# New spacings in a kernel's own planner, and a list of dense items in another order

## The chip, the cores and the metric

One core of one Trainium2 chip runs the whole program. The time is device microseconds of one execution, as a median over several runs. A profile is one execution of its own; its views give times in us from the span's start. TensorE is also called PE, VectorE DVE, ScalarE ACT, GpSimd POOL, SyncE SP.

## The reference

Two layers of a transformer over 256 latent tokens and 256 context tokens of 1024 channels, in float32. Cut to what matters here:

```python
for l in range(DEPTH):                                   # DEPTH = 2
    m_lat, m_ctx = (cond @ w_mod[l] + b_mod[l] for cond in (silu(c), silu(c_ctx)))   # 6 x 1024 each
    h = modulate(rmsnorm(x or ctx, norm1_g[l]), shift1, scale1)
    p = h @ w_in[l]          # q, k, v of three mixers, and 3 x 1024 gates
    ya = attention(GQA, 8 heads of 64 on 2 key heads, rotary)
    yb = neighbourhood attention (8 heads, bias) ; context keys in the same softmax
    yc = attention(MLA, 8 heads, keys and values from a latent of 256)
    y = (g0 * (ya @ w_o_gqa) + g1 * (yb @ w_o_na) + g2 * (yc @ w_o_mla)) @ w_out[l]
    x = x + gate1 * y
    x = x + gate2 * (square(relu(modulate(rmsnorm(x, norm2_g[l]), shift2, scale2) @ w_mlp1[l])) @ w_mlp2[l])
    # the context tokens go the same way in layer 0 alone
return rmsnorm(x, final_norm_g)
```

Latent queries read latent and context keys, context queries read context keys alone. Layer 1 computes only the latent stream to its end.

## The kernel before

**Matmuls.** A float32 product is made of three matmuls of fp32r operands: each operand is split into a high part (a cast on ACT) and a low part (a subtraction on DVE), and `mm3` (L762 to L764) adds high·high, high·low and low·high in one PSUM bank. Activations are stored transposed, channels on partitions; a contraction over 1024 channels is eight chunks of three matmuls. In layer 0 most have 512 columns (latent and context tokens), in layer 1 256.

**Weights** lie in DRAM as tiles of 128 x 1024, in the order of their use. SP issues one DMA per tile into a raw buffer (three of their own, `raw`, and others lent from the arena of slots, `s`); ACT casts it into `wh` (L699), DVE makes `wl` (L700), and the raw buffer is free again. There are three pairs of `wh` and `wl` (wh_69 with wl_70, wh_71 with wl_72, wh_73 with wl_74); an item called "more" lends further pairs from the arena, "less" takes them back.

**Modulation.** The 16 half tiles of shift and scale of layer 0's first norm (items c0 to c7) are used by TensorE straight from the raw buffer (L835), with a selecting matmul behind each pair (L845); chunk c of the normalized input waits for item c. The other 80 tiles (items w) are reduced by DVE (L905).

**Attention.** A unit is a pair of heads: four of neighbourhood attention (NA), four of MLA, four of GQA per layer, in this order. For every half of 128 queries a job makes scores (L1524, L1525; for MLA L762 to L764 with 96 rows), a maximum (L1639 to L1651), an exponential on ACT (L1667), a scaling on DVE or ACT (L1678 or L1676, whichever the planner finds free first), four transposes (L1696), a cast and a subtraction (L808, L809), and then the group's weighted sum (L1730, L1731). MLA's heads are put together by DMAs on POOL's queue (L1405, L1407, L1409).

**What sets the order.** The program is built by a planner. `SEQ` names, for each layer, the dense items in the order in which they get their slots and weights: qN, kN, vN, aN, lN, ckv, rope are projections for NA, GQA and MLA, gXN and oXN gate and output tiles of a mixer, yX and sX its result buffers and their splitting, "attn" gives attention its buffers, "norm", W and M are the second norm, the output projection and the MLP. Every item and every attention job is a coroutine that asks for an engine with a cost in us. The planner keeps its own rough clock: when an engine is free in it, the waiting request with the best key is issued, and so stands next in that engine's queue. The chip's queues run in that order, each stopping at an instruction whose inputs are not there. A cost does nothing else than to move instructions. The costs and the hop between engines:

```python
    def post(self, th, cmd):
        ...
            key = (th.pri, th.order, self.seq) if e == "pe" else (self.now + slack, th.order, self.seq)
    def dispatch(self):
        ...
                cost = w[1] * (2 if e == "pe" and self.now < COLD else 1)
                self.busy[e] = self.now + cost
```

On TensorE attention's jobs come ahead of dense items (`pri` −1 against 1), and dense items fill what is left.

Of the kernel before, what the change touches and what calls it, by code (L numbers as in the profile page):

```python
# [30 lines left out]
GA, NA, ML = range(3)  # L31
# [34 lines left out]

BR = {"N": NA, "L": ML, "G": GA}
SEQ = (
# [7 lines left out]
)  # L76


# [314 lines left out]

class Planner:
    ENGINES = ("pe", "act", "dve", "pool", "hw", "dma")
    HOP = 0.15

    def __init__(self):
        self.now, self.seq = 0.0, 0
# [40 lines left out]
    def step(self, th, val=None):  # L440
        while True:
            try:
                cmd = th.gen.send(val)
            except StopIteration:
                self.live -= 1
                self.threads.remove(th)
                return
            val = None
            th.cmd = cmd
            k = cmd[0]  # L450
            if k in self.pend or k == "any":
                hop = self.HOP if th.eng != k else 0.0
                th.eng = k
                self.at(self.now + hop, lambda: self.post(th, cmd))
                return
            if k == "wait":
                if not cmd[1].on:
                    th.eng = None
                    cmd[1].waiters.append(th)
                    return  # L460
            elif k == "get":
                self.seq += 1
                cmd[1].waiters.append((th.pri, th.order, self.seq, th, cmd[2]))
                self.serve(cmd[1])
                return
            elif k == "sleep":
                th.eng = None
                self.at(self.now + cmd[1], lambda: self.step(th))
                return
            else:  # L470
                raise ValueError(k)
# [73 lines left out]
class Prog:  # L545
# [138 lines left out]
    def transfer(self, n):  # L684

        yield ("sleep", 0.65)
        yield ("dma", n * 1.422e-3, lambda: None)
        yield ("sleep", 1.2)

    def arrive(self, i, r, n):  # L690
# [75 lines left out]
    def acc(self, out, a, b):  # L766

        def get(o):
            if isinstance(o, Opnd):
                yield from o.wait()  # L770
                return o.hi, o.lo
            if callable(o):
                return (yield from o())
            return o

        n = 1
        for d in out.shape[1:]:
            n *= d
        for k in range(len(a)):
            x = yield from get(a[k])  # L780
            y = yield from get(b[k])
            yield ("pe", 3 * max(n, 256) / 2400.0 + (0.0128 if n <= 256 else 0.0093),
                   lambda: self.mm3(out, x, y, k == 0, k == len(a) - 1))

    @staticmethod
# [104 lines left out]
    def it_wm(self, l, part, fc, mem):  # L890
# [11 lines left out]
        for j in range(nj):  # L902
            for h in range(2):
                r = slice(h * 512, (h + 1) * 512)
                yield from self.dve(512, lambda: nc.vector.tensor_tensor_reduce(  # L905
                    self.junk, w[0][:, r], self.crow[j][:, r], 1.0, 0.0, ALU.mult, ALU.add,
                    accum_out=acc[1][:, fc, j, h:h + 1]), SL_M)
        self.give_raw(w)
# [710 lines left out]
    def job(self, l, g, qt, qleaf):  # L1619
# [7 lines left out]
        def score():  # L1627
            if lat:
                make(sc, slice(qt * P, qt * P + P), slice(0, T))
            else:  # L1630
                for a in range(2):
                    make(sc[:, a * 256:(a + 1) * 256], slice(NLAT + a * P, NLAT + a * P + P), slice(NLAT, T))
        yield ("pe", 0.645 if br == ML else 0.43, score)
        for f in qleaf:
            f.done()
        sm = self.pool_c.tile([P, 6], F32, tag="sm", bufs=8, name=self.nm("sm"))
# [4 lines left out]
        elif br == NA:  # L1641
# [4 lines left out]
            def mx():  # L1646
# [2 lines left out]
                nc.vector.tensor_scalar(pt[:, 256:512], sc[:, 256:512], 1.0, None, ALU.mult, ALU.max,  # L1649
                                        accum_out=sm[:, 5:6])  # L1650
                nc.vector.tensor_scalar(sm[:, 0:1], sm[:, 4:5], sm[:, 5:6], -1.0, ALU.max, ALU.mult)  # L1651
            yield ("dve", 0.9, mx)
            src = pt
            self.bias_n[h] = self.bias_n.get(h, 0) + 1
            if self.bias_n[h] == 2:
# [8 lines left out]
        def ex():  # L1664
            for a in range(m):
                r = slice(a * w, (a + 1) * w)
                nc.scalar.activation(pt[:, r], src[:, r], AF.Exp, bias=sm[:, a:a + 1], accum_out=sm[:, 2 + a:3 + a])  # L1667
        yield ("act", 0.62 + 0.15 * (m - 1), ex)
        if src is sc:
            self.unbank(bank)  # L1670

# [21 lines left out]
        def tr():  # L1693
# [3 lines left out]
            else:  # L1697
                for c in range(2):
                    for a in range(2):
                        nc.tensor.transpose(ps[:, c * 256 + a * P:c * 256 + (a + 1) * P],  # L1700
                                            pt[:, a * 256 + c * P:a * 256 + (c + 1) * P], self.ident)
        yield ("pe", 0.443, tr)
        self.pl.give(self.pbuf, pt)
        hi, lo = g["prob"]
        if lat:
# [11 lines left out]
    def pv(self, l, g):  # L1717
# [9 lines left out]
        for k0 in range(0, nk, 2):  # L1727
            def fn():
                for k in (k0, k0 + 1):
                    mm(ps, v[o + k], hi[:, k, :], start=k == 0, stop=False)  # L1730
                    mm(ps, v[o + k], lo[:, k, :], start=False, stop=k == nk - 1)  # L1731
            yield ("pe", 0.443, fn)
        self.pl.give(self.prob, g["prob"])
        for f in g["vleaf"]:
            f.done()
# [436 lines left out]
```

## Time and profile before

| | |
|---|---|
| median of 3 runs | 1458.03 us (1457.59 to 1458.78) |
| the profiled execution | 1459.33 us, span 1457.6, granted clock 0.991 |
| PE, DVE, ACT busy | 97%, 74%, 52% of the span |
| DMA | 210.91 MB, mean 145 GB/s |

A row of grouped instructions gives line, engine, operation, operands by the program's names, shape and count; a timeline's row start, length and, in brackets, the idle time before it with what ended it; a row of stretches each engine's busy time with its number of instructions. TensorE's work follows the list: the start to about 45 us, layer 0's projections and units to about 420, its output projection, norm and MLP to about 850, and the same for layer 1, whose units lie between 965 and 1190 and whose second norm is near 1257.

### The profile page before, as it was taken

Reading aid. Unit: us, or ns where it says so; the run is one execution under the profiler, and the core shown is the slowest. Engines: PE = TensorE matmul, PEld = TensorE weight load, DVE = VectorE, ACT = ScalarE, POOL = GpSimd, SP = SyncE. Lnnn points to the kernel's source line nnn. Section 1 sums busy time; section 2 is a strip of 40 time slices with the busy share of each in tenths; the row PEclk is TensorE's granted clock in tenths of the full one; section 3 lists DMA queues with packets and bytes.
Section 4 is the critical chain, followed back from the end, with each engine's and each line's share of the span. In section 5 each row is a group of like instructions: output and inputs, shape, how many; then the busy total and the mean of one; then the engine's idle time right before and its main releaser. Section 6 shows DMA issues by size and latency. Waiting matters only on the chain.

```text
span 1457.6 us, 23967 instructions
## 1 busy us (share of the span) xinstructions
PE 1419.6 (97%) x9294; PEld 1290.2 (89%) x9294; DVE 1076.7 (74%) x2236; ACT 752.9 (52%) x1374; POOL 34.8 (2%) x74
## 2 busy tenths in 40 slices
PE   5999999999999999999999999998999999999997
PEld 3899889988888899888888889987998999999997
DVE  5638886768986988889766457647688887766665
ACT  4538886547842344223232244447667874645543
POOL 0000100000000000000000000000011000000000
PEclk8999999999999999999999999999999999999999
DMA  8511432342334553565656434333256336455551
GB/s 311 183 63 56 123 87 75 131 145 72 116 118 143 174 171 119 162 199 189 201 189 201 131 116 155 115 121 114 94 140 178 119 120 227 145 188 182 180 187 45
DMA packets 61779, 210.91 MB, mean 145 GB/s; under 512 B 7392, under 2 KB 9440, under 8 KB 61664
## 3 DMA queue, kind: packets, MB, share of 16 engines
q1 hardware_dynamic: 56448, 197.94, 41.1%
q0 software_dynamic: 4352, 10.49, 3.2%
q8 instruction: 73, 1.20, 0.3%
q10 hardware_dynamic: 864, 0.93, 0.2%
q14 instruction: 42, 0.34, 0.1%
HBM read 200.95 MB, written 1.05 MB: 139 GB/s over the span
## 4 chain that ended last, share of the span: by engine, by line
PE 89%; DVE 5%; DMA 3%; ACT 2%; issue 1%; POOL 0%; ACTq 0%; SPq 0%; DVEq 0%; POOLq 0%
PE b L762 26%; PE b L763 26%; PE b L764 26%; PE b L1696 2%; PE b L1731 2%; DMA s<-s 2%; PE b L1730 2%; DVE wl L700 1%; PE b L1524 1%; PE b L1525 1%; ACT s L1667 1%; DVE s L809 1%; DMA raw<-in_wts_dram 1%; PE b L1700 1%; PE b L835 1%
## 5 line engine op out<-in xcount | busy, mean ns | idle before, releaser
L762 PE MATMUL b<-s,wh 128*128 128x256 f32 (+1 forms) x1704 | 579.4, 340 | 3.1 <-ACT wh L699 1.9
L764 PE MATMUL b<-s,wl 128*128 128x256 f32 (+1 forms) x1704 | 571.6, 335 | 1.8 <-DVE wl L700 1.8
L763 PE MATMUL b<-s,wh 128*128 128x256 f32 (+1 forms) x1704 | 571.7, 335 | 0.1
L699 ACT CAST wh<-raw 128x1024 fp32r<-128x1024 f32 (+1 forms) x198 | 204.3, 1034 | 349.2 <-PE b L763 285.9
L762 PEld LDWEIGHTS b<-s,wh 128*128 128x128 f32 x1704 | 324.7, 191 | 37.1 <-ACT wh L699 2.7
L764 PEld LDWEIGHTS b<-s,wl 128*128 128x128 f32 x1704 | 324.5, 190 | 35.8 <-DVE wl L700 3.2
L763 PEld LDWEIGHTS b<-s,wh 128*128 128x128 f32 x1704 | 324.9, 191 | 30.4 <-DVE s L1048 0.4
L700 DVE TENSOR_TENSOR wl<-raw,wh 128x1024 fp32r<-128x1024 f32 (+1 forms) x198 | 237.4, 1201 | 138.3 <-ACT wh L699 136.9
L905 DVE CUSTOM_DVE_ANT_0 s<-raw,s 128x512 f32<-128x512 f32 x236 | 162.6, 689 | 13.8 <-DMA raw<-in_wts_dram 9.3
L762 PE MATMUL b<-s,s 128*128 128x256 f32 (+4 forms) x520 | 154.3, 297 | 2.3 <-DMA s<-s 2.3
L763 PE MATMUL b<-s,s 128*128 128x256 f32 (+4 forms) x520 | 153.0, 294 | 0.0
L764 PE MATMUL b<-s,s 128*128 128x256 f32 (+4 forms) x520 | 152.9, 294 | 0.0
L809 DVE TENSOR_TENSOR s<-b,s 128x512 fp32r<-128x512 f32 (+3 forms) x151 | 100.4, 674 | 17.7 <-ACT s L808 16.7
L762 PE MATMUL b<-wh,s 128*128 128x256 f32 x368 | 106.0, 288 | 0.0
L1860 DVE SCALAR_TENSOR_TENSOR s<-b,mod,s 128x256 f32<-128x256 f32 x120 | 55.4, 482 | 66.2 <-PE b L764 66.0
L764 PE MATMUL b<-wh,s 128*128 128x256 f32 x368 | 104.1, 283 | 0.0
L763 PE MATMUL b<-wl,s 128*128 128x256 f32 x368 | 104.0, 283 | 0.0
L762 PEld LDWEIGHTS b<-s,s 128*128 128x128 f32 (+1 forms) x520 | 99.4, 191 | 3.8 <-issue 1.7
L764 PEld LDWEIGHTS b<-s,s 128*128 128x128 f32 (+1 forms) x520 | 99.4, 191 | 2.0
L763 PEld LDWEIGHTS b<-s,s 128*128 128x128 f32 (+1 forms) x520 | 99.5, 191 | 1.1
L808 ACT CAST s<-b 128x512 fp32r<-128x512 f32 (+3 forms) x151 | 85.4, 578 | 28.2 <-PE b L764 11.8
L699 ACT CAST wh<-s 128x1024 fp32r<-128x1024 f32 x35 | 36.7, 1049 | 72.6 <-PE b L763 64.4
(156 smaller groups left out, 1897.6 us busy)
## 6 DMA issues: line engine op xcount, KB each, us to landing
raw<-in_wts_dram SPq DMA_DIRECT2D x301, 512.0 KB, 3.6
s<-in_wts_dram SPq DMA_DIRECT2D x59, 512.0 KB, 4.2
s<-in_xT_dram SPq DMA_DIRECT2D x16, 256.0 KB, 3.9
s<-s POOLq DMA_DIRECT2D x28, 128.0 KB, 4.7
s<-in_bias_dram POOLq DMA_DIRECT2D x16, 192.0 KB, 2.6
s<-s POOLq DMA_DIRECT2D x12, 256.0 KB, 4.2
raw<-in_wts_dram SPq DMA_DIRECT2D x4, 432.0 KB, 4.0
raw<-in_wts_dram SPq DMA_DIRECT2D x4, 384.0 KB, 3.0
```

The source lines that it names most:

```text
L699: yield from self.act(n, lambda: nc.scalar.copy(hi[:, :n], r[0][:, :n]), SL_W)
L700: yield from self.dve(n, lambda: nc.vector.tensor_tensor(lo[:, :n], r[0][:, :n], hi[:, :n].bitcast(F32), ALU.subtract), SL_W)
L762: mm(out, a[0], b[0], start=start, stop=False)
L763: mm(out, a[0], b[1], start=False, stop=False)
L764: mm(out, a[1], b[0], start=False, stop=stop)
L808: yield from self.act(n, lambda: nc.scalar.copy(hi, src), slack)
L809: yield from self.dve(n, lambda: nc.vector.tensor_tensor(lo, src, hi.bitcast(F32), ALU.subtract), slack)
L905: yield from self.dve(512, lambda: nc.vector.tensor_tensor_reduce(self.junk, w[0][:, r], self.crow[j][:, r], 1.0, 0.0, ALU.mult, ALU.add, ...
L1696: nc.tensor.transpose(ps[:, c * P:(c + 1) * P], pt[:, c * P:(c + 1) * P], self.ident)
L1730: mm(ps, v[o + k], hi[:, k, :], start=k == 0, stop=False)
L1731: mm(ps, v[o + k], lo[:, k, :], start=False, stop=k == nk - 1)
L1860: yield from self.dve(NLAT, lambda: nc.vector.scalar_tensor_tensor(o, bank.ap[:, i * NLAT:(i + 1) * NLAT], g[:, c, j:j + 1], x, ALU.mult, ...
```

## The change

The costs that the planner reckons with get other values, and `SEQ` lists the items in another order. In the costs: a step from TensorE or ACT to another engine is 0.22 or 0.17 us and not 0.15; a group of three matmuls of 256 columns 0.360 and not 0.333 us, of 512 columns 0.680 and not 0.649; a weight tile's transfer 1.28 and not 1.46 us; DVE's reduction of half a modulation row 0.73 and not 0.60; scores, maxima, exponentials, transposes and weighted sums as shown. What the program computes, its instructions' shapes and its buffers stay.

```diff
 SEQ = (
-    "start less c0 yN k1 c2 c3 c1 k2 c5 c7 c6 raw2 q0 c4 q1 more4 rope v1 k0 yL v0 q3 ckv w attn q2 l1 k3 l0 l3 "
...
+    "start c2 k0 c4 c0 q1 c6 c1 k1 k2 raw2 c7 c3 yL more4 q0 rope less c5 v1 v0 q3 ckv w attn yN q2 l1 k3 l0 l3 "
...
-    "w q2 w q1 ckv q0 rope v1 v0 k2 w w k1 w w a0 k0 w yN w k3 w q3 attn a2 w gL0 l0 yL l1 a1 gL1 gN0 drop l2 w w "
...
+    "w q0 rope w v0 q1 q2 ckv yN w attn k0 v1 k2 w w k1 a0 w k3 w q3 w a2 gN3 l0 w l1 gN0 w yL a1 gG2 drop gG7 w "
...
-    HOP = 0.15
+    HOP = {"pe": 0.22, "act": 0.17}
...
-                hop = self.HOP if th.eng != k else 0.0
+                hop = self.HOP.get(th.eng, 0.15) if th.eng != k else 0.0
...
-        yield ("dma", n * 1.422e-3, lambda: None)
+        yield ("dma", n * (1.25e-3 if n > 512 else 1.45e-3), lambda: None)
...
-            yield ("pe", 3 * max(n, 256) / 2400.0 + (0.0128 if n <= 256 else 0.0093),
+            yield ("pe", 3 * (max(n, 256) / 2400.0 + 0.0134),
...
-                yield from self.dve(512, lambda: nc.vector.tensor_tensor_reduce(
+                yield ("dve", 0.73, lambda: nc.vector.tensor_tensor_reduce(
...
-        yield ("pe", 0.645 if br == ML else 0.43, score)
+        yield ("pe", (0.72 if br == ML else 0.47) if lat else (0.74 if br == ML else 0.49), score)
...
-            yield ("dve", 0.9, mx)
+            yield ("dve", 1.06, mx)
...
-        yield ("act", 0.62 + 0.15 * (m - 1), ex)
+        yield ("act", 0.68 + 0.23 * (m - 1), ex)
...
-        yield ("pe", 0.443, tr)
+        yield ("pe", 0.385, tr)
...
-            yield ("pe", 0.443, fn)
+            yield ("pe", 0.50, fn)
```

The hop is looked up by `th.eng`, the engine that the coroutine leaves.

Three places of the built program show what moves. The first is ACT's queue in layer 1, where the key tiles of NA (items k) are cast and their products copied out (L1183, L1192: the heads of a key pair, `s` a slot, `b` a PSUM bank). Before:

```order
L699 CAST wh_69<-raw_67 128x1024
L1183 CAST s_7867<-b_79 64x512 x4
L1192 CAST s_7868<-s_7868 64x512 x2
L699 CAST wh_73<-raw_66 128x1024
L1183 CAST s_7946<-b_77 64x512 x4
L1192 CAST s_7947<-s_7947 64x512 x2
L699 CAST wh_73<-raw_68 128x1024
L1183 CAST s_8044<-b_78 64x512 x4
L1192 CAST s_8060<-s_8060 64x512 x2
L1667 ACT_TABLE_LOAD
L1667 ACTIVATE s_8139,sm_8438<-s_8139,sm_8438 128x512
L699 CAST wh_73<-raw_67 128x1024
```

and now:

```order
L699 CAST wh_73<-raw_67 128x1024
L2033 DMA gag_8439<-in_gains_dram 128x128
L1183 CAST s_8016<-b_78 64x512 x4
L1739 COPY s_7756<-b_82 64x256
L1192 CAST s_8026<-s_8026 64x512 x2
L699 CAST wh_69<-raw_68 128x1024
L1183 CAST s_8027<-b_76 64x512 x4
L1192 CAST s_8056<-s_8056 64x512 x2
L699 CAST wh_71<-raw_67 128x1024
L699 CAST wh_73<-raw_68 128x1024
```

Three casts that went into one buffer, wh_73, one after the other, now go through three buffers in turn, and a weighted sum's copy (L1739) already stands among them.

The second place is TensorE's queue in layer 1's first unit, from a job's transposes to the weighted sum of their group. Before (the group of bank b_78):

```order
L1696 MATMUL b_75<-ident,s_8139 128x128 x4
L1524 MATMUL b_76<-s_7946,s_7191 128x512
L1525 MATMUL b_76<-s_7947,s_7191 128x512
L1730 MATMUL b_78<-s_8065,s_7865 128x256
L1731 MATMUL b_78<-s_8138,s_7865 128x256
```

and now (the group of bank b_82):

```order
L1696 MATMUL b_75<-ident,s_2370 128x128 x4
L762 MATMUL b_78<-s_6933,wh_73 128x512
L763 MATMUL b_78<-s_6933,wh_73 128x512
L764 MATMUL b_78<-s_6933,wl_74 128x512
L762 MATMUL b_78<-s_6934,wh_73 128x512
L763 MATMUL b_78<-s_6934,wh_73 128x512
L764 MATMUL b_78<-s_6934,wl_74 128x512
L762 MATMUL b_76<-s_6766,wh_69 128x512
L763 MATMUL b_76<-s_6766,wh_69 128x512
L764 MATMUL b_76<-s_6766,wl_70 128x512
L1730 MATMUL b_82<-s_7852,s_7709 128x256
L1731 MATMUL b_82<-s_7853,s_7709 128x256
```

Where two score matmuls stood between them, nine dense ones stand now.

The third place is TensorE's queue at the start, around the last two halves of modulation (L835; item c4 before, c5 now). Before:

```order
L835 MATMUL b_78<-raw_67,s_110 32x256 x4
L762 MATMUL b_76<-s_114,wh_71 128x512
L763 MATMUL b_76<-s_114,wh_71 128x512
L764 MATMUL b_76<-s_114,wl_72 128x512
L835 MATMUL b_78<-s_129,s_110 32x256 x4
```

and now:

```order
L835 MATMUL b_81<-s_130,s_110 32x256 x4
L762 MATMUL b_82<-s_116,wh_69 128x512
L763 MATMUL b_82<-s_116,wh_69 128x512
L764 MATMUL b_82<-s_116,wl_70 128x512
L762 MATMUL b_82<-s_117,wh_69 128x512
L763 MATMUL b_82<-s_117,wh_69 128x512
L764 MATMUL b_82<-s_117,wl_70 128x512
L762 MATMUL b_76<-s_116,wh_71 128x512
L763 MATMUL b_76<-s_116,wh_71 128x512
L764 MATMUL b_76<-s_116,wl_72 128x512
L835 MATMUL b_81<-raw_67,s_110 32x256 x4
```

Ahead of the last half stood 18 dense matmuls, and 36 stand there now; on SP's queue its tile was the 19th weight and is now the 24th.

10 rows, old and new, of the table SEQ are left out of this document.

## The prediction

> **What bounds the kernel now.** I read the page first, then busy time by stretch, then TensorE's own waits, then the order of time around the longest of them. The page's busy shares and its chain of waits:
>
> ```profile
> PE 1419.6 (97%) x9294; PEld 1290.2 (89%) x9294; DVE 1076.7 (74%) x2236; ACT 752.9 (52%) x1374; POOL 34.8 (2%) x74
> ...
> PE 89%; DVE 5%; DMA 3%; ACT 2%; issue 1%; POOL 0%; ACTq 0%; SPq 0%; DVEq 0%; POOLq 0%
> ```
>
> TensorE is the bound: 1457.6 − 1419.6 leaves 38.0 us without a matmul, and the change leaves the matmuls as they are (9152 in the program before and after, the same number of each shape). So the most that an order can win is what TensorE loses. Busy time by stretch (from:to, length, then busy time and count of PE, weight loads, DVE, ACT, POOL, the granted clock, DMA share, GB/s) says where:
>
> ```profile
> 0.00:40.00 40.00, 24.88 (x174) 15.98 (x175) 22.76 (x52) 16.95 (x29) 1.22 (x10) 0.87 0.87 308
> 100.00:200.00 100.00, 99.76 (x640) 89.25 (x639) 83.65 (x223) 80.21 (x184) 11.25 (x22) 1.00 0.34 95
> 300.00:400.00 100.00, 99.56 (x553) 84.98 (x553) 85.63 (x182) 71.22 (x149) 0.00 (x0) 1.00 0.32 106
> 600.00:700.00 100.00, 100.00 (x443) 82.81 (x442) 91.46 (x203) 30.05 (x38) 0.00 (x0) 1.00 0.59 189
> 1200.00:1300.00 100.00, 97.32 (x783) 96.47 (x783) 72.82 (x123) 50.88 (x80) 0.00 (x0) 0.97 0.56 189
> 1300.00:1400.00 100.00, 100.00 (x835) 100.00 (x835) 63.35 (x86) 47.91 (x67) 0.00 (x0) 1.00 0.56 182
> 1400.00:1458.00 58.00, 50.18 (x420) 49.89 (x418) 33.62 (x56) 23.92 (x41) 0.00 (x0) 0.96 0.29 97
> ```
>
> The start loses 15.1 us, the end 7.8, layer 1's second norm 2.7, layer 0's attention (100 to 400) 0.7. The MLPs lose nothing; they also give the spacing of matmuls: 100/443 = 0.226 us at 512 columns (600 to 700), 100/835 = 0.120 at 256 (1300 to 1400). What is left lies in layer 1's attention, in finer stretches:
>
> ```profile
> 960.00:980.00 20.00, 19.05 (x117) 16.81 (x115) 8.37 (x14) 8.77 (x13) 0.00 (x0) 1.00 0.33 107
> 980.00:1000.00 20.00, 16.85 (x80) 13.01 (x81) 13.85 (x40) 15.13 (x26) 1.07 (x2) 1.00 0.48 159
> 1000.00:1020.00 20.00, 17.05 (x106) 15.44 (x105) 17.79 (x69) 15.79 (x34) 1.61 (x3) 0.83 0.30 97
> 1020.00:1040.00 20.00, 19.03 (x150) 17.98 (x149) 17.23 (x56) 16.70 (x37) 0.54 (x1) 1.00 0.19 63
> 1060.00:1080.00 20.00, 18.44 (x136) 17.29 (x135) 14.39 (x27) 12.32 (x27) 3.30 (x6) 1.00 0.74 185
> 1100.00:1120.00 20.00, 17.75 (x131) 16.55 (x130) 16.91 (x40) 16.99 (x34) 3.14 (x6) 1.00 0.65 178
> ```
>
> From 960 to 1040 TensorE stands idle 0.95 + 3.15 + 2.95 + 0.97 = 8.0 us, and at a clock of 0.83 it loses another 0.17 × 17.05 = 2.9: 10.9 us in 80. TensorE's own waits name the releasers (sum, times, longest):
>
> ```profile
> PE b L762 <- DMA s<-s: 2.3, 2, 1.6
> PE b L1730 <- ACT s L808: 2.3, 1, 2.3
> PE b L762 <- ACT wh L699: 1.9, 2, 1.0
> PE b L764 <- DVE wl L700: 1.8, 3, 0.7
> PE b L1731 <- DVE s L809: 1.7, 3, 0.8
> PE b L1696 <- ACT s L1676: 1.5, 1, 1.5
> ```
>
> **Term A, layer 1's first attention units.** Two faults show there. The first is the weights. Rows around 987 us (start, length, idle before it and its releaser), of ACT, TensorE and DVE:
>
> ```profile
> 986.38 1.04 ACT L699 CAST wh<-raw 128x1024 fp32r<-128x1024 f32 x1 [1.98 <-PE b L763]
> 987.48 0.50 PE L762 MATMUL b<-s,wh 128*128 128x512 f32 x1 [0.95 <-ACT wh L699]
> 987.46 1.22 DVE L700 TENSOR_TENSOR wl<-raw,wh 128x1024 fp32r<-128x1024 f32 x1 [1.29 <-ACT wh L699]
> 988.74 0.50 PE L764 MATMUL b<-s,wl 128*128 128x512 f32 x1 [0.53 <-DVE wl L700]
> ```
>
> The cast waited for TensorE to finish with the buffer, TensorE then for the cast, and then for DVE's low half: one buffer pair for three tiles in a row, as the order on ACT shows (wh_73, wh_73, wh_73). In the change the same tiles go through wh_73, wh_69, wh_71, so a cast runs a tile ahead: eight groups of three matmuls, 24 × 0.226 = 5.4 us, against 1.04 + 1.22 of conversion. These waits go wholly. The second fault is attention itself:
>
> ```profile
> 1003.58 0.60 PE L1696 MATMUL b<-ident,s 128*128 128x128 f32 x4
> 1006.92 0.58 PE L1730 MATMUL b<-s,s 128*128 128x256 f32 x1 [2.27 <-ACT s L808]
> 1008.18 0.58 PE L1731 MATMUL b<-s,s 128*128 128x256 f32 x1 [0.67 <-DVE s L809]
> ```
>
> A transpose is followed by two score matmuls (0.45 us of work) and then by the weighted sum that needs ACT's and DVE's copies of it. In the change nine dense matmuls stand there: 9 × 0.226 = 2.03. I call such covering work a cushion, and counted it from the order for every wait of TensorE in layer 1's attention (its work between the last matmul that the awaited chain needs and the matmul that waits, at the spacings above). Before, 7 cushions lie under 1 us, all within 20 us of matmuls around the first unit; in the change none, the least there being 1.63. The cause is the place of "attn" in the list: the first four units now begin some 20 us of matmul work earlier and are spread over 62 us of it, not 39. What stays I take from 100 to 200 us, where the same kind of units in layer 0, with cushions from 1.7 up, lose 0.24 in 100 us: 0.7 with room for two or three short waits. A = −(10.9 − 0.7) = **−10.2**, from −10.9 (all) to −5 (half of the waits move on).
>
> The clock belongs to that term. It stood at 0.83 around an idle stretch of 2.27 + 0.67 us, and at 1.00 from 980 to 1000, where single gaps are 0.95 at most; so one such gap left over would cost its 2.3 and the 2.9 as well, and A would be −10.2 + 2.3 + 2.9 = −5.0, the bound again. [...]
>
> **Term B, the wait of transposes for ACT L1676**, 1.5 us near 1108: the cushion was 1.78 us, at the same place now 2.14 and over: −1.2, from −1.5 to 0.
>
> **Term C, the moved heads of MLA in layer 1.** Their scores wait for three DMAs in a row on POOL's queue:
>
> ```profile
> 1098.46 0.49 POOL L1409 DMA_DIRECT2D s<-s x1 [1.35 <-DMA s<-s]
> ...
> 1103.96 0.47 PE L762 MATMUL b<-s,s 96*128 96x512 f32 x1 [0.72 <-DMA s<-s]
> ```
>
> The last of them took 5.5 us to its user. From the split that feeds the DMAs to the scores stand 13.7 us of matmuls before and 13.9 now for the second pair of heads (its wait was 1.6), 13.8 and 12.5 for the third (0.7). The third loses 1.3 of cover: C = **+1.1**, from 0 to +4 (all four pairs 1 us worse).
>
> **Term D, the last units (GQA).** Waits with a cushion under 2.25 us go from 8 to 19, under 1.75 from 1 to 4. Layer 0 has 55 of the first kind for 0.7 idle us, 0.013 each; at 0.07 each the 11 new ones are +0.8, from 0 to +3.
>
> **Term E, the start.** Its end is set by the last of 16 modulation tiles. Rows of two stretches, of SP's issues, of the last tile's matmuls, and of the median time from issue to landing:
>
> ```profile
> 24.00:28.40 4.40, 2.07 (x15) 1.17 (x15) 4.40 (x12) 1.93 (x4) 0.00 (x0) 0.85 0.88 292
> 28.40:37.00 8.60, 8.37 (x53) 4.51 (x53) 6.19 (x15) 2.53 (x6) 0.00 (x0) 0.50 0.85 312
> ```
> ```profile
> 36.02 1.18 SPq L681 DMA_DIRECT2D s<-in_wts_dram  x2
> ...
> 42.87 3.87 SPq L681 DMA_DIRECT2D s<-in_wts_dram  x2
> ```
> ```profile
> 42.17 0.64 PE L835 MATMUL b<-s,s 128*32 128x256 f32 x8
> ```
> ```profile
> s<-in_wts_dram SPq DMA_DIRECT2D x59, 512.0 KB, 4.2
> ```
>
> Counted along SP's queue, the last modulation tile is the 19th weight before (issued 36.02, used 42.17) and the 24th now, since chunk 5 moved behind q0 and the three rope tiles. The 24th was issued at 42.87; 4.2 us on it would come at 47.1, 4.9 later. Ahead of it TensorE now has 18 more dense matmuls, 18 × 0.226 = 4.1, and the rope tiles ahead are 768 of 3072 columns short, 0.75 of a tile at 6.85/5 = 1.37 us, 1.0. 4.9 − 4.1 − 1.0 is −0.2, nothing at this accuracy. Both bounds come from the half clock: 8.37 × 0.5 = 4.2 us either won or lost a second time. E = **0**, −4 to +4.
>
> **The rest.** Layer 0's units: cushions under 1.75 us go from 8 to 7: −0.3, ±1. Layer 1's norm and the end keep their chains (cushions 0 before and now): 0, ±0.5. The constants (HOP, transfer, the spacings) are used while the program is built and issue nothing. 15 scalings and copies go from ACT to DVE (1216 to 1201 and 2204 to 2219 instructions in the order). At the mean of DVE's scaling,
>
> ```profile
> L1678 DVE TENSOR_SCALAR s<-s,sm 128x512 f32<-128x512 f32 x53 | 25.4, 484 | 1.0
> ```
>
> 484 ns, they are 7.3 us spread over attention's 300 and more, under TensorE's matmuls, and 7.3 at most if nothing covered them.
>
> Sum: −10.2 − 1.2 + 1.1 + 0.8 + 0 − 0.3 = −9.8. The profiled execution took 1459.33 us (1.7 around its span); the runs' median, 1458.03, is 1.3 lower, so the median comes to **1448.2**.
>
> **Rivals.** *Half of the waits move on* (A at −5, D at +3): 1458.0 − 5 − 1.2 + 1.1 + 3 − 0.3 = 1455.6, near no change. For it: from 1000 to 1040 DVE is busy 35 of 40 us, and the units still need it; against: they are spread over 62 us now. *The cushions are too thin* ends slower: a cast of weights at the head of ACT's queue waits for TensorE (1.98 us in the row of 986.38) and holds up the softmax behind it, and this befalls the 27 waits of layer 1 that have under 2.25 us. At 0.36 us each (9.8/27) the win is gone, at 0.6 each the time is 1448.2 + 16.2 = 1464. Against it: layer 0's 55 at 0.013. *The start wins its clock back*: 1448.2 − 4.2 = 1444.0; for it, the long gap before 28.4 (2.3 us) is split in two or three in the new order; against, it stays bound by DMA at a share of 0.88. *The corrected clock changes nothing that TensorE waits for*, since 97% busy leaves it little: 1458; the order shows otherwise in the quoted places.
>
> **How the numbers follow.** Forecast 0.64 (alone 1445 to 1453), start's clock 0.15, half of the waits 0.09, no effect 0.05, too thin 0.07. A measurement of this kernel tells a change from none at about 0.2%, 2.9 us: faster is under 1455.1, slower over 1460.9. Faster takes the first two and half of the third: 0.84; same 0.09; slower 0.07. The range to hold 8 in 10 is 1441 to 1456.
>
> **What would show it.** Right: from 960 to 1040 (now the units lie some 20 us earlier, so 930 to 1030 as well) TensorE idle under 1.5 us and the clock at 1.00; no wait of L762 or L764 for L699 or L700 in layer 1; the 2.3 of L1730 gone; the wait for DMA at 3 to 4 us. The MLPs' 443 and 835 per 100 us must stay. It is wrong if a gap over 2 us stands in those units, if TensorE idles over 17 us before 48, or if L1696, L1524 and L1730 together wait over 5 us after 1080.

## The result, and the profile after

The changed kernel takes **1448.5 us** (median of 4 runs, 1447.45 to 1452.61) where the kernel before takes 1458.4 (4 runs): a ratio of 0.9938, 95% interval 0.9918 to 0.9958. On another chip, five rounds gave 1448.94 against 1456.6, ratio 0.9942 (0.9930 to 0.9955). The profiled execution is the slowest of the first four, 1452.61 us with a span of 1450.8; a second profile, taken with the experiments and called "change, again" below, has 1448.68 and 1446.8.

Busy shares and chain of the changed kernel's page; the work of TensorE is the same, the span 6.8 us shorter:

```profile
PE 1418.5 (98%) x9294; PEld 1290.5 (89%) x9294; DVE 1081.8 (75%) x2251; ACT 746.6 (51%) x1359; POOL 34.7 (2%) x74
...
PE 86%; DVE 6%; DMA 4%; ACT 2%; issue 1%; POOL 0%; ACTq 0%; SPq 0%; DVEq 0%; POOLq 0%
```

Its busy time by stretch (from:to, length, busy time and count of PE, weight loads, DVE, ACT, POOL, granted clock, DMA share, GB/s):

```profile
0.00:40.00 40.00, 23.53 (x175) 15.44 (x176) 24.37 (x55) 18.34 (x31) 1.22 (x10) 0.91 0.89 324
600.00:700.00 100.00, 99.73 (x440) 82.29 (x439) 87.08 (x196) 30.24 (x38) 0.00 (x0) 1.00 0.56 181
930.00:950.00 20.00, 20.00 (x165) 19.98 (x164) 10.00 (x20) 7.24 (x13) 0.42 (x1) 1.00 0.32 112
950.00:970.00 20.00, 20.00 (x148) 19.04 (x147) 7.43 (x15) 7.72 (x17) 0.00 (x0) 1.00 0.20 65
970.00:990.00 20.00, 20.00 (x138) 18.46 (x138) 17.31 (x50) 15.07 (x26) 1.07 (x2) 1.00 0.46 145
990.00:1010.00 20.00, 20.00 (x121) 17.69 (x120) 16.74 (x52) 15.51 (x28) 0.54 (x1) 1.00 0.61 194
1010.00:1030.00 20.00, 19.88 (x156) 18.95 (x155) 18.80 (x67) 18.14 (x40) 1.61 (x3) 1.00 0.33 103
1090.00:1110.00 20.00, 16.85 (x105) 15.66 (x104) 14.24 (x30) 10.99 (x20) 4.20 (x8) 0.83 0.69 175
1200.00:1300.00 100.00, 97.07 (x785) 96.33 (x784) 72.73 (x120) 51.13 (x79) 0.00 (x0) 0.97 0.55 185
1300.00:1400.00 100.00, 100.00 (x836) 100.00 (x835) 63.57 (x87) 48.00 (x69) 0.00 (x0) 1.00 0.56 184
1400.00:1451.00 51.00, 43.45 (x363) 43.06 (x361) 29.76 (x51) 21.12 (x37) 0.00 (x0) 0.96 0.25 84
```

Layer 1's first units, where 8.0 us of idle time and 2.9 of clock were lost, now lose 0.12 in 100 us at full clock. One hole is left in the units: 3.15 us and a clock of 0.83 from 1090 to 1110. TensorE's waits name it:

```profile
PE b L835 <- DMA raw<-in_wts_dram: 13.7, 4, 12.1
PE b L762 <- DMA s<-s: 3.1, 1, 3.1
PE b L845 <- ACT s L841: 2.3, 2, 1.7
PE b L969 <- ACT s L945: 1.9, 2, 1.2
...
PE b L1731 <- DVE s L809: 0.3, 1, 0.3
```

It is the third pair of MLA heads. The waits for L699, L700, L808 and L1676 are gone; L969 (the norms) waits for L945 where none was listed before.

### The profile page after: what moved, and what is told of

Its sections match the earlier page's. It is cut to its first block, busy times and chain, and to the rows that moved or that the text cites. A ratio compares the mean times of both kernels' runs of the same rounds, so it can differ in the third digit from the quotient of the medians.

```text
span 1450.8 us, 23974 instructions
## 1 busy us (share of the span) xinstructions
PE 1418.5 (98%) x9294; PEld 1290.5 (89%) x9294; DVE 1081.8 (75%) x2251; ACT 746.6 (51%) x1359; POOL 34.7 (2%) x74
## 4 chain that ended last, share of the span: by engine, by line
PE 86%; DVE 6%; DMA 4%; ACT 2%; issue 1%; POOL 0%; ACTq 0%; SPq 0%; DVEq 0%; POOLq 0%
PE b L763 25%; PE b L762 25%; PE b L764 25%; PE b L1696 3%; DMA raw<-in_wts_dram 3%; PE b L1731 2%; PE b L1730 2%; DVE wl L700 1%; PE b L1524 1%; PE b L1525 1%; DMA s<-s 1%; DVE s L905 1%; DVE s L1044 1%; DMA s<-in_wts_dram 1%; PE b L1700 1%
## 5 line engine op out<-in xcount | busy, mean ns | idle before, releaser
L762 PE MATMUL b<-s,wh 128*128 128x256 f32 (+1 forms) x1664 | 566.5, 340 | 1.2 <-ACT s L1047 1.1
L763 PE MATMUL b<-s,wh 128*128 128x256 f32 (+1 forms) x1664 | 561.4, 337 | 0.9 <-DVE s L1905 0.3
L764 PE MATMUL b<-s,wl 128*128 128x256 f32 (+1 forms) x1664 | 559.8, 336 | 0.0
L699 ACT CAST wh<-raw 128x1024 fp32r<-128x1024 f32 (+3 forms) x184 | 188.4, 1027 | 341.8 <-PE b L763 290.1
L762 PEld LDWEIGHTS b<-s,wh 128*128 128x128 f32 x1664 | 317.7, 191 | 34.0 <-ACT s L1047 1.4
L763 PEld LDWEIGHTS b<-s,wh 128*128 128x128 f32 x1664 | 317.8, 191 | 33.3 <-DVE s L1048 1.7
L764 PEld LDWEIGHTS b<-s,wl 128*128 128x128 f32 x1664 | 317.4, 191 | 32.5
L700 DVE TENSOR_TENSOR wl<-raw,wh 128x1024 fp32r<-128x1024 f32 (+3 forms) x184 | 218.8, 1191 | 103.9 <-ACT wh L699 100.1
L762 PE MATMUL b<-s,s 128*128 128x256 f32 (+4 forms) x568 | 169.5, 298 | 3.1 <-DMA s<-s 3.1
L763 PE MATMUL b<-s,s 128*128 128x256 f32 (+4 forms) x568 | 167.8, 295 | 0.0
L764 PE MATMUL b<-s,s 128*128 128x256 f32 (+4 forms) x568 | 167.5, 295 | 0.0
L762 PEld LDWEIGHTS b<-s,s 128*128 128x128 f32 (+1 forms) x568 | 109.0, 192 | 4.8 <-issue 3.3
L764 PEld LDWEIGHTS b<-s,s 128*128 128x128 f32 (+1 forms) x568 | 109.0, 192 | 2.5
L763 PEld LDWEIGHTS b<-s,s 128*128 128x128 f32 (+1 forms) x568 | 109.2, 192 | 1.4
L809 DVE TENSOR_TENSOR s<-b,s 128x512 fp32r<-128x512 f32 (+3 forms) x151 | 100.1, 670 | 13.1 <-ACT s L808 12.1
L762 PE MATMUL b<-wh,s 128*128 128x256 f32 (+1 forms) x360 | 104.0, 289 | 0.0
L764 PE MATMUL b<-wh,s 128*128 128x256 f32 (+1 forms) x360 | 102.1, 284 | 0.0
L763 PE MATMUL b<-wl,s 128*128 128x256 f32 (+1 forms) x360 | 102.1, 284 | 0.0
L808 ACT CAST s<-b 128x512 fp32r<-128x512 f32 (+2 forms) x151 | 85.0, 577 | 22.1 <-PE b L764 9.1
L699 ACT CAST wh<-s 128x1024 fp32r<-128x1024 f32 x45 | 47.2, 1049 | 67.9 <-PE b L763 59.0
```

Source lines behind the costliest of these rows:

```text
L699: yield from self.act(n, lambda: nc.scalar.copy(hi[:, :n], r[0][:, :n]), SL_W)
L700: yield from self.dve(n, lambda: nc.vector.tensor_tensor(lo[:, :n], r[0][:, :n], hi[:, :n].bitcast(F32), ALU.subtract), SL_W)
L762: mm(out, a[0], b[0], start=start, stop=False)
L763: mm(out, a[0], b[1], start=False, stop=False)
L764: mm(out, a[1], b[0], start=False, stop=stop)
L808: yield from self.act(n, lambda: nc.scalar.copy(hi, src), slack)
```

## The experiments

Two measures stand beside the times. The first is TensorE's idle time from 960 to 1040, which holds layer 1's first units in every kernel. The second is **lost time**: the time that has passed at a matmul, less the work of the matmuls before it at the spacings of the prediction (some 1380 us in all, the same for every kernel); it counts idle time and slow clock alike. The table counts from the first matmul on; the wait for the first tiles, 10.9 to 12.1 us, is in none of its rows. The start's row is good for comparing kernels, less so for its level, since the spacings were taken from matmuls of other shapes. The row "layer 1: norm" runs up to the first unit.

| us lost | before | change | again | k0 early | change, k0 late | by cushions |
|---|---|---|---|---|---|---|
| start | 17.5 | 17.7 | 19.3 | 19.9 | 19.7 | 16.7 |
| layer 0: units | 10.0 | 10.4 | 10.6 | 9.7 | 10.3 | 9.9 |
| layer 0: second norm, MLP | 0.9 | 3.0 | 3.2 | 1.2 | 2.9 | 1.2 |
| layer 1: norm | 1.3 | 2.7 | 2.7 | 1.3 | 5.5 | 1.6 |
| layer 1: first units | 16.7 | 2.1 | 2.9 | 7.0 | 12.2 | 2.9 |
| third pair of MLA | 2.9 | 6.4 | 0.7 | 2.5 | 1.3 | 0.3 |
| other units | 2.3 | 2.1 | 2.2 | 2.3 | 2.2 | 1.9 |
| second norm, end | 15.2 | 15.2 | 15.4 | 15.0 | 14.4 | 14.3 |

Between the two profiles of the change most rows repeat to a few tenths, the first units to 0.8; the start (16.7 to 22.6 over thirteen profiles), MLA's third pair (6.4 and 0.7) and the clock behind a gap (0.83 behind 2.27 us in the kernel before, 0.91 behind 2.28 with attn moved) do not.

### Costs and list apart

The list for both layers with the old costs; then the new costs with the old list.

```diff
-    "start less c0 yN k1 c2 c3 c1 k2 c5 c7 c6 raw2 q0 c4 q1 more4 rope v1 k0 yL v0 q3 ckv w attn q2 l1 k3 l0 l3 "
...
+    "start c2 k0 c4 c0 q1 c6 c1 k1 k2 raw2 c7 c3 yL more4 q0 rope less c5 v1 v0 q3 ckv w attn yN q2 l1 k3 l0 l3 "
...
-    "w q2 w q1 ckv q0 rope v1 v0 k2 w w k1 w w a0 k0 w yN w k3 w q3 attn a2 w gL0 l0 yL l1 a1 gL1 gN0 drop l2 w w "
...
+    "w q0 rope w v0 q1 q2 ckv yN w attn k0 v1 k2 w w k1 a0 w k3 w q3 w a2 gN3 l0 w l1 gN0 w yL a1 gG2 drop gG7 w "
...
```

> The kernel before with the new list for both layers and its old costs. If the list carries the gain, TensorE's waits of L762 and L764 for L699 and L700 in layer 1 and the 2.3 us of L1730 are gone as in the change (counted from the order, no cushion of the first units under 1 us, but two of layer 1's last units at 0.45 and 0.50 us, and 12 instead of 7 under 1.75 in layer 0): 1450 us, 1448 to 1453. If the list only works together with the clock it was arranged for, 1455 or more.

Measured: 1455.75 us against 1456.6, ratio 0.9991 (0.9977 to 1.0005). No gain, though the first units are right: TensorE is busy 78.12 of the 80 us. The stretch of the first units, and that of the last (GQA):

```profile
960.00:1040.00 80.00, 78.12 (x539) 71.94 (x538) 66.97 (x201) 59.70 (x113) 3.22 (x6) 1.00 0.39 126
1140.00:1160.00 20.00, 16.90 (x105) 14.70 (x104) 16.98 (x32) 15.19 (x33) 0.00 (x0) 0.83 0.33 105
```

Three transposes wait there, and the clock falls behind them, to 0.83 as the mean of that stretch (rows of the order of time: start, length, in brackets the idle time before it):

```profile
1148.82 0.63 PE L1696 MATMUL b<-ident,s 128*128 128x128 f32 x4 [0.64 <-DVE s L1678]
1151.13 0.76 PE L1696 MATMUL b<-ident,s 128*128 128x128 f32 x4 [1.23 <-DVE s L1678]
1153.86 1.11 PE L1696 MATMUL b<-ident,s 128*128 128x128 f32 x4 [1.11 <-ACT s L1676]
```

The loss of the units outside the first ones and the third MLA pair is 8.8 us here, 2.2 in the change. So the same list under another clock of the planner makes another order: the first units keep their cushions, the last ones lose theirs (the two of 0.45 and 0.50 us that the expectation names). The list has to be judged with the costs it is played under.

```diff
-    HOP = 0.15
+    HOP = {"pe": 0.22, "act": 0.17}
...
```

> The kernel before with the new costs and its old list for both layers. If the list carries the gain: first units with 5 cushions under 1 us instead of 7, so part of the 10.9 us lost there at most comes back: 1456 us, 1454 to 1459. If the truer clock carries it, since it places jobs where TensorE does not wait, 1449 to 1452.

Measured: 1467.43, ratio 1.0078 (1.0059 to 1.0096), slower by more than either theory had. First units 14.2 us lost, 3.0 at layer 0's second norm, 12.7 in layer 0's units. Truer costs by themselves win nothing.

### The layers apart

New costs, the old list in one layer and the new in the other. First, from the change, layer 0 back:

```diff
-    "start c2 k0 c4 c0 q1 c6 c1 k1 k2 raw2 c7 c3 yL more4 q0 rope less c5 v1 v0 q3 ckv w attn yN q2 l1 k3 l0 l3 "
...
+    "start less c0 yN k1 c2 c3 c1 k2 c5 c7 c6 raw2 q0 c4 q1 more4 rope v1 k0 yL v0 q3 ckv w attn q2 l1 k3 l0 l3 "
...
```

> The change with layer 0's old list (and so the old start); costs and layer 1's list are new. If the gain is all in layer 1's first units: 1446 to 1448 us, a little under the change, since in the change's trace the start lost 0.8 us more than before, layer 0's second norm 1.5 more and a row near 698 us 0.5. If layer 0 and the start had given part of the gain, 1450 to 1454. The third pair of MLA heads in layer 1 has the same 12.5 us of cover as in the change: a wait for DMA of 3 us and a granted clock near 0.83 there would show that the change's is no chance of one execution; under 1 us that it is.

Measured: 1450.31, ratio 0.9958 (0.9942 to 0.9974). The interval overlaps the change's; the 1446 to 1448 did not come. In the profile the start lost 21.2 us and layer 0's units 12.0. The second is no chance of one execution: with the costs alone, that is the same costs and the same list of layer 0, it was 12.7, against 9.7 to 10.6 in the table. So layer 0's new list gives back 1 to 2 us that the new costs take there. The stretch of the third MLA pair, with the change's own order there:

```profile
1090.00:1110.00 20.00, 19.62 (x144) 18.49 (x144) 18.94 (x42) 15.12 (x27) 4.38 (x9) 1.00 0.86 215
```

No gap, full clock: the change's 3.15 us are one execution's.

Then, from the change, layer 1 back:

```diff
-    "w q0 rope w v0 q1 q2 ckv yN w attn k0 v1 k2 w w k1 a0 w k3 w q3 w a2 gN3 l0 w l1 gN0 w yL a1 gG2 drop gG7 w "
...
+    "w q2 w q1 ckv q0 rope v1 v0 k2 w w k1 w w a0 k0 w yN w k3 w q3 attn a2 w gL0 l0 yL l1 a1 gL1 gN0 drop l2 w w "
...
```

> The change with layer 1's old list; costs, layer 0's list and the start are new. If the gain is all in layer 1's list: 1457 to 1461 us, since the waits of the first units (5 cushions under 1 us) stay and layer 0 loses 2 to 3 us more. If layer 0 and the start had given part of it, 1453 to 1455.

Measured: 1465.75, ratio 1.0059 (1.0044 to 1.0075). So the gain is layer 1's list, under the new costs. The time lies over 4 us above the expectation. In the profile (1464.1 us) the start lost 22.6, some 3 to 5 us more than in the change; but all five executions lie between 1462.8 and 1466.8, and whether their starts lost as much is not known.

### What moves the first units

The prediction named the place of "attn". That was tried alone:

```diff
-    "w q2 w q1 ckv q0 rope v1 v0 k2 w w k1 w w a0 k0 w yN w k3 w q3 attn a2 w gL0 l0 yL l1 a1 gL1 gN0 drop l2 w w "
+    "w q2 w q1 ckv q0 rope v1 v0 k2 w w k1 w w a0 k0 w yN attn w k3 w q3 a2 w gL0 l0 yL l1 a1 gL1 gN0 drop l2 w w "
...
```

> The kernel before with attn alone moved, to behind yN, some 11 items earlier in layer 1's list. The prediction names the place of attn as the cause; by that the units would begin earlier and 5 us or more would be won: 1453 us or less. But in the order the units stand where they stood, only slots have other numbers: by that nothing is won, 1455.5 to 1458.

Measured: 1455.91, ratio 0.9996 (0.9984 to 1.0008): nothing. TensorE's stretch is as before (71.98 there):

```profile
960.00:1040.00 80.00, 71.79 (x455) 63.40 (x454) 57.63 (x177) 56.60 (x107) 3.22 (x6) 0.98 0.32 102
```

Then k0, the key tile that unit 0 waits for (a unit starts when its queries, keys and values are there, and units start in order):

```diff
-    "w q2 w q1 ckv q0 rope v1 v0 k2 w w k1 w w a0 k0 w yN w k3 w q3 attn a2 w gL0 l0 yL l1 a1 gL1 gN0 drop l2 w w "
+    "w q2 w q1 ckv q0 rope v1 v0 k0 k2 w w k1 w w a0 w yN w k3 w q3 attn a2 w gL0 l0 yL l1 a1 gL1 gN0 drop l2 w w "
...
```

> The kernel before (old costs, old list of layer 0) with one item of layer 1's list moved: k0, the first key tile of NA, stands ahead of k2 and not behind a0. In the order the first unit then begins 6 us of matmul work earlier, the first four spread over 26 us and not 20, and of the 7 cushions under 1 us one is left (0.45 us, a low half). If the place of k0 sets the two faults, and not that of attn or the new costs: 1448 to 1452 us where the kernel before has 1456.6, and the stretch of matmul work around the first units loses under 4 us where it lost 14. If the gain needs the costs or the rest of the list: 1455 to 1458.

Measured: 1449.46, ratio 0.9946 (0.9933 to 0.9960). One moved item, with the old costs, gives the time of the whole change, though not in the same places: the first units lose 7.0 us, where under 4 were expected and the change loses 2.1 to 2.9, and the norms lose nothing more. Its stretch of the first units, and the longest waits that are left:

```profile
960.00:1040.00 80.00, 76.48 (x514) 68.86 (x513) 64.05 (x192) 56.73 (x108) 3.23 (x6) 1.00 0.37 120
```

```profile
PE b L1696 <- ACT s L1676: 2.2, 3, 1.2
PE b L764 <- DVE wl L700: 1.9, 2, 1.5
```

The other way round, in the change:

```diff
-    "w q0 rope w v0 q1 q2 ckv yN w attn k0 v1 k2 w w k1 a0 w k3 w q3 w a2 gN3 l0 w l1 gN0 w yL a1 gG2 drop gG7 w "
+    "w q0 rope w v0 q1 q2 ckv yN w attn v1 k2 w w k1 a0 k0 w k3 w q3 w a2 gN3 l0 w l1 gN0 w yL a1 gG2 drop gG7 w "
...
```

> The changed kernel with one item of layer 1's list moved back: k0 behind a0, as it stood before. In the order the faults of the kernel before return: five cushions under 1 us in the first units (0.23 and 0.45 us, twice each, at weights that go three in a row through one pair), units 20 us of matmul work later. If the place of k0 carries the gain: the first units lose 10 us or more again, 1456 to 1461 us. If the rest of the list or the costs carry it: 1448 to 1451.

Measured: 1464.67, ratio 1.0048 (1.0031 to 1.0065). Both faults are back; its stretch, then its waits:

```profile
960.00:1040.00 80.00, 71.78 (x455) 62.04 (x455) 55.66 (x166) 55.89 (x105) 3.23 (x6) 1.00 0.33 107
```

```profile
PE b L762 <- ACT wh L699: 2.5, 3, 1.1
PE b L1696 <- ACT s L1676: 2.2, 3, 1.4
PE b L764 <- DVE wl L700: 2.0, 2, 1.5
```

It came out slower than the kernel before and than the 1456 to 1461 expected. Part of that is in the profile: the first units lost 12.2 us, layer 0's norm keeps the change's loss, and of the 5.5 us in the row of layer 1's norm 1.3 are more waits for L699 and L700, at 963 us, behind the norm. The profiled execution is the fastest of the six, though (1460.05 us at a mean clock of 0.994; the others have 1463.5 to 1466.9 at 0.989 to 0.991), and what the others lose besides was not profiled.

And k0 early under the new costs, from the kernel with these and the old list:

```diff
-    "w q2 w q1 ckv q0 rope v1 v0 k2 w w k1 w w a0 k0 w yN w k3 w q3 attn a2 w gL0 l0 yL l1 a1 gL1 gN0 drop l2 w w "
+    "w q2 w q1 ckv q0 rope v1 v0 k0 k2 w w k1 w w a0 w yN w k3 w q3 attn a2 w gL0 l0 yL l1 a1 gL1 gN0 drop l2 w w "
...
```

> The new costs with the old list in which k0 alone stands ahead of k2. The new costs with the old list took 1467. If k0's place is the cause under either costs: the first units lose 4 to 7 us where they lost 13, 1457 to 1462 us; what is left over the kernel before comes from the other places that the new costs move (layer 0's units and its second norm, MLA's second pair of heads with 11.1 us of cover). If k0's place works only with the old costs: 1465 or more.

Measured: 1458.2, ratio 1.0004 (0.9992 to 1.0015), where the same costs with k0 behind a0 had 1.0078; the first units lost 8.0 (4 to 7 were expected), not 14.2. So k0 works under either costs. From the order, its place should act in two ways. Behind a0 it comes after k2 and k1, so when it arrives the next units' keys are there already and the units follow each other closely; and a0's two weight tiles keep two of the three pairs until a2 has given out slots, so k0 and the tiles behind it go through one pair. The second was tried by moving a0 and leaving k0 behind the rest:

```diff
-    "w q2 w q1 ckv q0 rope v1 v0 k2 w w k1 w w a0 k0 w yN w k3 w q3 attn a2 w gL0 l0 yL l1 a1 gL1 gN0 drop l2 w w "
+    "w q2 w q1 ckv q0 rope v1 v0 k2 w w k1 w w k0 w yN w k3 w q3 attn a2 a0 w gL0 l0 yL l1 a1 gL1 gN0 drop l2 w w "
...
```

> The kernel before with one other item moved: a0 (two weight tiles that keep two of the three pairs until a2's slots are given) stands behind a2. In the order the run of one pair is gone, but units come as close together as before (4 cushions under 1 us, at transposes and weighted sums). If the two faults add: the waits of L762 and L764 for L699 and L700 go (3.7 us in all before), the waits of L1696, L1730 and L1731 stay with the slow clock behind them: 1452 to 1455 us. If the weights were the root of the second fault too (a cast that waits holds up the softmax): 1447 to 1450.

Measured: 1454.58, ratio 0.9985 (0.9974 to 0.9995). The waits for L699 and L700 are gone from the list of waits, but a transpose takes over:

```profile
PE b L1696 <- ACT s L1676: 6.5, 3, 4.5
```

```profile
960.00:1040.00 80.00, 71.71 (x464) 64.80 (x463) 57.15 (x178) 57.47 (x107) 3.23 (x6) 0.96 0.30 95
```

As long as the first units stand close, their softmax is what TensorE waits for; taking the weights' wait away moves most of it there. That the distance of the units is the other half of k0's effect is argued from this; it was not moved alone.

### A list arranged by cushions alone

From the kernel before (old costs, layer 0 as it was), items of layer 1's list were moved until the cushions, counted in the order, were as thick as they would get. No time went into it.

```diff
-    "w q2 w q1 ckv q0 rope v1 v0 k2 w w k1 w w a0 k0 w yN w k3 w q3 attn a2 w gL0 l0 yL l1 a1 gL1 gN0 drop l2 w w "
+    "w w q1 ckv v0 q0 rope k0 q2 k2 v1 w w k1 w w a0 w yN w k3 q3 w attn a2 gL0 l0 w yL l1 a1 gL1 drop gN0 w l2 w "
...
```

> The kernel before with its costs and its layer 0, and a list for layer 1 that was arranged by counting cushions alone, from the list with k0 early: no cushion under 1.68 us in layer 1's attention, 20 under 2.25 where the change has 33; the third pair of MLA heads has 13.8 us of cover. If the time follows cushions: the first units lose under 1.5 us (6.5 with k0 early alone), and the norm after layer 0 keeps the 1.2 us of the kernel before where the change has 2.6 to 3.3: 1442 to 1446 us, under the change. If there is something else in the first units that takes their place: 1448 to 1451.

Measured: **1443.41 us** (1441.44 to 1445.26), ratio 0.9908 (0.9892 to 0.9923), under the change's 0.9942 (0.9930 to 0.9955) with no overlap. The first units lose 2.9 us, more than the 1.5 that were expected and about as much as in the change; what it has over both profiles of the change are mainly the norms, which keep about the losses of the kernel before (1.2 and 1.6), and a start that lost less. In this list k0 stands early and "attn" late. Its first units, and the stretch of the third MLA pair:

```profile
960.00:1040.00 80.00, 79.77 (x571) 74.63 (x571) 66.16 (x194) 62.32 (x119) 3.75 (x7) 1.00 0.42 133
1090.00:1110.00 20.00, 20.00 (x152) 18.94 (x151) 19.67 (x45) 18.17 (x41) 1.02 (x2) 1.00 0.54 142
```

### The change again

The changed kernel, without an edit, beside the others.

> The changed kernel again, beside the others. If its first profile's wait of 3.1 us for DMA at the third pair of MLA heads, and the slow clock behind it, is part of its order: again 3 us and a granted clock near 0.83 from 1090 to 1110, and 1450 us or more beside 1456.6 before. If it is one execution's: under 1 us, as the same order in layer 1 had it with layer 0's old list, and 1447 to 1449.

Measured: 1448.94, ratio 0.9942. The third MLA pair waits 0.4 us in this execution, at full clock:

```profile
1090.00:1110.00 20.00, 19.62 (x143) 18.43 (x142) 19.50 (x44) 15.65 (x29) 4.17 (x8) 1.00 0.75 196
```

## Why the prediction was right, and where not

**The time.** 1448.2 was forecast, 1448.5 came, through a sum whose parts were partly off in opposite directions; that they cancelled to 0.3 us is luck. By lost time the two profiles of the change stand 6.7 and 10.7 us under the kernel before: first units −14.6 and −13.8, third MLA pair +3.5 and −2.2, norms +3.5 and +3.7, the start +0.2 and +1.8, the wait before the first matmul +0.3 and −0.9, each other row +0.6 at most.

**Term A** (−10.2): right in size and mechanism. Counted as there (idle time, and what the clock takes of the busy time), 960 to 1040 lost 10.9 us before and 0.12 after. The change's row for it:

```profile
960.00:1040.00 80.00, 79.88 (x556) 74.01 (x555) 67.82 (x199) 63.69 (x120) 3.22 (x6) 1.00 0.42 130
```

So −10.8, a little over the forecast. (The −14 of lost time reach to about 1100 us, past the second MLA pair.) **The step that failed is its cause**: "the place of attn in the list". Moved alone it gave 0.9996; k0 moved alone gave 0.9946, and moved back in the change 1.0048; and the list by cushions has first units as good as the change's with "attn" late. The order of the built program already said so: with attn moved, TensorE's first units stood where they had stood.

**Term B** (−1.2): the 1.5 us for L1676 near 1108 are gone from the waits, and did not turn up in another place. They count with the third MLA pair in the table, as does most of term C.

**Term C** (+1.1, 0 to +4): the mechanism and the pair of heads were right, and it is no fixed sum. In the first profile the wait for DMA goes from 2.3 to 3.1, and the clock at 0.83 takes 0.17 × 16.85 = 2.9 more: +3.7. In the second the wait is 0.4, and in layer 1's list with layer 0's old one there is no gap either. This one gap is about what the profiled execution lies above the three others (3.5 to 5.2 us).

**Term D** (+0.8): nothing to see. The other units lost 2.3 before and 2.1 and 2.2 now, so cushions between 1.7 and 2.25 us cost under the 0.07 each that was taken. The rival behind it is real, and its point lies lower: in the new list under the old costs two cushions of 0.45 and 0.50 us, with some near 1.2, cost 6.6 us at one place.

**Term E** (0): right, idle and clock together 15.1 + 0.13 × 24.88 = 18.4 before, 16.5 + 0.09 × 23.53 = 18.6 after. (The clock's column leaves out the half pace of the first matmuls, up to about 20 us in both: eight modulation matmuls take 1.08 us at 11.82 (before) and 12.12 (after), and 0.64 at 37.53 and 37.77; see the last section.) The last modulation tile was expected near 47.1 us and ran at 46.99.

**The rest** ("0, ±0.5" for the norms) was too small, and is the term that was mis-sized: layer 0's second norm and MLP lose 3.0 and 3.2 us where they lost 0.9, layer 1's norm 2.7 where it lost 1.3, together +3.5 and +3.7. "Keep their chains (cushions 0 before and now)" looked at the chains and not at what stands beside them. In layer 1's first norm L969 now waits 0.7 us for L945, near 918 us, where nothing waited. (Its other 1.2 us lie in the second norm near 1250 and take the place of 0.9 that L967 waited for L950; that row stays at 15.2.) In layer 0 TensorE is idle for only 0.7 us from 500 to 850, in short waits for L1905 and L1048; what else makes up the 2 us there stays open. The first units' gain over the forecast and, in the second profile, a short wait at the third pair cover it. No run moved a norm alone, but the kernels show where the idle time comes from. From 500 to 850 us it is nothing with the old costs and the old list of layer 0, 0.4 with the new list, 1.65 with the new costs and 0.7 with both. From 850 to 950 it is 0.8 in the change, 0.25 with its list and the old costs, and nothing with layer 1's old list under either costs.

**The rivals.** "Half of the waits move on" did not come in the change, but it did in the kernel with a0 late. "Too thin" came in the new list with the old costs. "The start wins its clock back" was not put to the test: no run shows its 4.2 us, and the last section says why the clock's column can't. "No effect" is out.

**The signs** asked for were there: under 1.5 us idle and full clock in the first units, no L762 or L764 behind L699 or L700, L1730's wait gone, 3.1 us for DMA in the profiled execution (0.4 in the other), 440 and 836 matmuls per 100 us in the MLPs.

## What to carry to other kernels

Where one engine is busy 97% of the time and the order is fixed when the program is built, the gain sits in a few places, and the work that lies between what a wait needs and the wait can be counted from the order without running it: here waits for ACT and DVE with more than about 1.7 us of such work cost nearly nothing (2.9 us lost in the first units of the list by cushions, whose thinnest is 1.68), and those under 1 us cost their idle time and then some (6.6 us, 2.98 of them idle, in the last units of the new list under the old costs, where two are 0.45 and 0.50). Waits for a chain of DMAs are another matter: the same 12.5 us of work left a wait of 3.1 us in one execution and of 0.4 in another. A planner's costs and the list that was arranged under them are one thing: changed apart, they gave nothing or a loss. And before a cause is named, undo that one thing alone: one item of the 187 in two rearranged lists, and not the one that was named, brought about two thirds of what the first units won.

## What the runs showed of the hardware

**The same gaps do not always cost the clock.** The kernels with the new costs and layer 1's old list have the same two gaps at weight tiles. First with layer 0's old list, the stretch and the rows:

```profile
980.00:1000.00 20.00, 16.32 (x62) 12.03 (x61) 11.74 (x21) 12.87 (x21) 0.00 (x0) 0.91 0.51 162
```

```profile
986.37 0.50 PE L762 MATMUL b<-s,wh 128*128 128x512 f32 x1 [1.12 <-ACT wh L699]
988.18 0.54 PE L764 MATMUL b<-s,wl 128*128 128x512 f32 x1 [1.08 <-DVE wl L700]
```

and with layer 0's new list:

```profile
980.00:1000.00 20.00, 16.32 (x69) 12.28 (x68) 11.74 (x21) 14.10 (x22) 0.00 (x0) 1.00 0.53 178
```

```profile
987.13 0.50 PE L762 MATMUL b<-s,wh 128*128 128x512 f32 x1 [1.12 <-ACT wh L699]
988.94 0.50 PE L764 MATMUL b<-s,wl 128*128 128x512 f32 x1 [1.08 <-DVE wl L700]
```

The clock is 0.91 in one and 1.00 in the other. The 2.27 us at L1730 gave 0.83 in the kernel before; with attn moved, the same wait of 2.28 us gave 0.91:

```profile
1000.00:1020.00 20.00, 16.84 (x113) 15.57 (x112) 18.32 (x75) 16.05 (x34) 1.61 (x3) 0.91 0.27 84
```

The granted clock is 0.50 in the slow part: 0.50 in each of the three stretches of 2 us from 1006.92 to 1012.92 in the kernel before; and with the new costs and both old lists the matmuls start 0.43 us apart from 988.52 to 991.51, and 0.23 apart before the gaps and after 991.93. So 20 × 0.17 / 0.5 = 6.8 us ran at half speed in the kernel before and 20 × 0.09 / 0.5 = 3.6 with attn moved, where stretches of 2 us (0.84, 0.50 and 0.81 from 1005.55 to 1011.55) give it finer, 0.64 + 2.00 + 0.76 = 3.4. Two gaps of 1.12 and 1.08 us, 0.7 us apart, were enough for such a part in the one kernel with layer 1's old list and gave none in the other; what decides it is not shown. For a price: in these four profiles a gap of 2.3 us, or two of 1.1 close together, cost the idle time and, with half speed over 0, 3.4 or 6.8 us, up to half of that on top: 0, 1.7 or 3.4 us.

**At the start the clock's column is not the pace.** With k0 early the column reads 1.00 for this stretch of the start, and TensorE is never idle in it:

```profile
24.00:48.00 24.00, 24.00 (x140) 15.03 (x133) 16.39 (x39) 10.31 (x17) 0.00 (x0) 1.00 0.83 302
```

Yet its matmuls of 512 columns start 0.43 us apart up to 41 us, and 0.23 apart behind it, as in the dense work of the MLPs:

```profile
39.96 0.63 PE L763 MATMUL b<-s,wh 128*128 128x512 f32 x1
40.39 0.63 PE L764 MATMUL b<-s,wl 128*128 128x512 f32 x1
40.82 0.63 PE L762 MATMUL b<-s,wh 128*128 128x512 f32 x1
...
43.16 0.40 PE L763 MATMUL b<-s,wh 128*128 128x512 f32 x1
43.40 0.39 PE L764 MATMUL b<-s,wl 128*128 128x512 f32 x1
```

So the column misses the half pace that this run begins with, and the rows have to be read. In the kernel before they show half pace up to about 20 us (eight modulation matmuls take 1.08 us at 17.19, and 0.64 at 20.59), which the column leaves out, and again from 27 to 37, which it has (0.50 from 28.40 to 37.00); with attn moved, once, up to about 30 us (40 matmuls in 6.00 busy us from 24 to 30, 47 in 4.46 from 30 to 36, and a column of 1.00 in both). These are the stretches of the two, then the last modulation tile of the second, which ran at 42.17 in the first:

```profile
24.00:48.00 24.00, 21.44 (x135) 13.81 (x136) 18.48 (x44) 11.08 (x19) 0.00 (x0) 0.79 0.86 303
```

```profile
24.00:48.00 24.00, 22.38 (x153) 14.46 (x146) 19.28 (x43) 11.11 (x19) 0.00 (x0) 1.00 0.89 322
```

```profile
40.87 0.64 PE L835 MATMUL b<-s,s 128*32 128x256 f32 x8
```

From the first matmul on, both run at half pace for about as long (some 19 us), and they lose about as much (17.5 and 17.0). The second's last tile is used 1.3 us earlier, and 0.6 of that is its first tile, which came at 11.2 and not at 11.8 us. So this pair says nothing of what a start at full pace would win. Over nine profiles the loss goes with the length of the half pace: 16.7 to 19.3 us in the five that had up to 19.4 us of it (the kernel before, both of the change, attn moved, by cushions), 19.7 to 22.6 in the four that had 22 to 30 (k0 early, k0 late, and the two with the layers apart). What decides that length, and how much of the loss it causes, stays open.
